# RG-LRU layer of a hybrid diffusion step on one core: unsplit float32 gates, the decay on ScalarE, a new pace table and x7 ahead of g6

## Chip, core and metric

The kernel runs on one core of a Trainium2 chip. The metric is the device time of one execution in microseconds, as the median of several runs. Engines are named as in the profile: PE (TensorE), PEld (its weight loads), DVE (VectorE), ACT (ScalarE), POOL (GpSimd), SP (SyncE, which issues most transfers).

## What is computed

One inference step of a two-layer backbone on 128 context and 512 latent tokens with 1024 channels. Layer 0 (SSD and differential attention) and both ConvFFNs are untouched. Layer 1 mixes with a bidirectional RG-LRU, all in float32:

```python
def rglru_direction(xr, wa, ba, wx, bx, lam, h0, reverse):
    xb = xr.reshape(b, n, RNN_BLOCKS, RNN_BLOCK_W)          # 16 blocks of 64 channels
    r = jax.nn.sigmoid(jnp.einsum('blnk,nkj->blnj', xb, wa).reshape(b, n, D_RNN) + ba)
    i = jax.nn.sigmoid(jnp.einsum('blnk,nkj->blnj', xb, wx).reshape(b, n, D_RNN) + bx)
    log_a = -RG_C * r * jax.nn.softplus(-lam)
    a = jnp.exp(log_a)
    u = jnp.sqrt(-jnp.expm1(2.0 * log_a)) * (i * xr)
    hseq, hlast = linear_scan(a, u, h0)                     # h[t] = a[t] h[t-1] + u[t]

def odd_mixer(h, w_in, conv_w, conv_b, wa, ba, wx, bx, lam, w_out, ctx):
    gate, xr = jnp.split(h @ w_in, 2, axis=-1)
    xr = dwconv_centred(xr, conv_w, conv_b)                 # width 4
    yf, hf = rglru_direction(xr, ..., h0f, False)
    yb, hb = rglru_direction(xr, ..., h0b, True)
    return ((yf + yb) * jax.nn.gelu(gate)) @ w_out, (hf, hb)
```

## The kernel before

Activations lie with channels on the 128 partitions and tokens on the free axis: 128 context tokens, a gap of 4 and 512 latent tokens make 644 columns (`NT`). The 1024 channels are 8 tiles. A float32 matrix product is done as three products of float32r parts (`mm3`): a weight and an operand are each split into a high part (a ScalarE cast) and a low part (a subtraction, for weights on GpSimd in pieces of 256 columns: the tiles `whi` and `wlo`, line 117), and high x high, high x low and low x high are added up in PSUM.

In the odd layer (`odd`) TensorE goes through 16 input projections, each of 8 x 2 x 3 = 48 products of 322 columns: for tile t the recurrent channels (called x0 to x7 here) and the gate channels (g0 to g7), in the order x0 g0 x1 g1 ... x7 g7 (`lru_order`). After an x block `recur` starts the tile's chain, after a g block `gelu`. Three weights are kept ready ahead of use.

The chain of a tile, for both directions d: the convolution `xr` (first tap on ScalarE, three on VectorE), its split into `xh` and `xl`, the split of the tile's gate weights `bd` into `bh` and `bl` (GpSimd), the gate products into the PSUM banks `mt` (two of them, 322 columns each), their Tanh on ScalarE into the tiles `t0` and `t1` (the profile calls both `t`), `decay` (Exp and Tanh on ScalarE, into `inv` and `t`), `forms` (five VectorE operations), `roots` (a square root on ScalarE, a product on GpSimd in three pieces), `scan` (one on VectorE for each direction), the addition of the two directions on GpSimd (three pieces, `pieces`, line 69), and `gated`, the product with the GELU. Most VectorE operations here go through one helper, line 317, so groups are told apart by tile names.

What runs when is set by ticks. `tick` is called as products are issued, once for each set of three in some loops and with 2 for each two sets in others, so a projection is 16 ticks; `after(n, f)` puts f into the program n ticks later. Every engine works off its instructions in the order in which the program issued them. The table `LRU` (and `LRU_LAST` for tile 7) holds the distances in ticks from the x block to the parts of its chain.

At the end of the layer `give_h` splits the gated tiles 0 to 6 into `H`, the operand of the output projection, as soon as the last gate block no longer needs H; the projection starts with the products that need H[0] to H[5], waits for H[6] and last for H[7].

Of the kernel before, what the change touches and what calls it, by code (L numbers as in the profile page):

```python
# [16 lines left out]
KD = D // 128  # L17
# [33 lines left out]
LRU_LAST = (9, 7, 14, 3, 7, 4, 4, 4)  # L51
LRU = (9, 9, 27, 3, 10, 7, 8, 6)
# [188 lines left out]
def tile_hybrid_step(ctx: ExitStack, tc: tile.TileContext, a, o):  # L241
# [184 lines left out]
    lru_order = [(what, t) for t in range(8) for what in "xg"]  # L426
# [1239 lines left out]
    def odd():  # L1666
        with ExitStack() as st:
# [35 lines left out]
            gys = {}  # L1703

            def recur(t, ps):

                xr = conv(pool, ps, "lru_cw", "lru_cb", 4, t, 8, "xr", 3)
                v = Core()

                def parts():  # L1710
                    v.xp = (pool.tile([128, NT], F32R, name="xh", tag="xh", bufs=2),
                            pool.tile([128, NT], F32R, name="xl", tag="xl", bufs=2))
                    split_into(v.xp, xr)

                def blocks():
                    b = bd[t % 2]
                    v.bh = pool.tile([128, 2, 2, 128], F32R, name="bh", tag="bh", bufs=2)
                    v.bl = pool.tile([128, 2, 2, 128], F32R, name="bl", tag="bl", bufs=2)
                    nc.scalar.copy(v.bh, b)
                    nc.gpsimd.tensor_sub(v.bl, b, v.bh.bitcast(F32))  # L1720
                    if t < 6:
                        gates_in(t + 2)

                hs = []

                def product(d, i):
                    if i == 0:
                        hs.append([])
                    w = tmp("t%d" % i, 4)
                    hs[d].append(w)  # L1730
                    for c0, c1 in HALVES:
                        ps = mtile()
                        mm3(ps, (v.bh[:, d, i], v.bl[:, d, i]), v.xp, c0, c1, 0, True, True)
                        nc.scalar.activation(w[:, c0:c1], ps[:, :c1 - c0], AF.Tanh, scale=0.5,
                                             bias=col(hba if i == 0 else hbx, d, t))

                def decay(d):
                    t1 = hs[d][0]
                    inv, e = tmp("inv", 2), tmp("e", 4)
# [21 lines left out]
                def scan(d):  # L1761
# [30 lines left out]
            def gelu(t, ps):  # L1792
                g = gys[t] = tmp("gy", 8)
# [167 lines left out]
```

## Time and profile before

| | |
|---|---|
| median of 3 runs | 2131.27 us (2123.99 to 2131.78) |
| profiled execution | 2128.0 us, span 2126.2 us |
| busy over the span | PE 1891.4 (89%), PEld 1735.7 (82%), DVE 1467.3 (69%), POOL 1208.1 (57%), ACT 964.2 (45%) |
| mean granted TensorE clock | 0.951 |
| HBM | 187.50 MB read, 6.92 MB written |

The shares are means over stages of different kinds. The odd layer lies between about 1322 and 1618 us of the span; times below are microseconds from the start of the span. A matmul's duration in the profile overlaps with the next one's, so the rate is read from the distance of two starts.

### The profile page before, as it was taken

What the parts mean: (1) busy time and instruction counts of PE and PEld (TensorE: products, weight loads), DVE (VectorE), ACT (ScalarE), POOL (GpSimd) and SP (SyncE); (2) the same over time, 40 slices, a digit from 0 to 9 for tenths busy, and PEclk for the clock granted to TensorE, in tenths of its full rate; (3) what the DMA queues carried; (4) which work ended last, traced back from release to release, by engine and by line L of the source; (5) the groups of instructions that cost most, each with busy time, mean ns of one, the idle gap of its engine ahead of it and who ended that gap; (6) DMA issues with size and microseconds to landing.
All of it is one profiled execution on the core that took longest, in us unless ns stands there. A gap on an engine that the chain in (4) does not pass through costs nothing.

```text
span 2126.2 us, 33767 instructions
## 1 busy us (share of the span) xinstructions
PE 1891.4 (89%) x12665; PEld 1735.7 (82%) x12665; DVE 1467.3 (69%) x2486; ACT 964.2 (45%) x1671; POOL 1208.1 (57%) x1542
## 2 busy tenths in 40 slices
PE   6878889999999988999999997977778799999997
PEld 4767768888888878799889997977678799999986
DVE  3477755656664357687777876788857778777874
ACT  3454444454553334343333444766724444343445
POOL 3335454333343535466666775688755577766772
PEclk9889999999999999999999998989789899999998
DMA  9545432121113431444542222111111122222221
GB/s 267 165 156 164 149 110 63 49 54 48 49 45 124 131 117 64 136 130 153 178 145 70 60 84 79 53 39 45 40 50 41 37 79 82 86 76 70 60 85 65
DMA packets 255578, 196.60 MB, mean 92 GB/s; under 512 B 13837, under 2 KB 233816, under 8 KB 255288
## 3 DMA queue, kind: packets, MB, share of 16 engines
q1 hardware_dynamic: 252664, 184.59, 28.9%
q0 software_dynamic: 2528, 7.13, 1.4%
q8 instruction: 100, 1.64, 0.3%
q10 hardware_dynamic: 224, 2.73, 0.3%
q14 instruction: 62, 0.51, 0.1%
HBM read 187.50 MB, written 6.92 MB: 91 GB/s over the span
## 4 chain that ended last, share of the span: by engine, by line
PE 36%; DVE 11%; POOL 9%; ACT 4%; issue 4%; DMA 4%; POOLq 0%; DVEq 0%; ACTq 0%; SPq 0%
PE wide L470 10%; PE wide L471 10%; PE wide L472 10%; POOL t L69 4%; POOL wlo L117 4%; DMA wraw<-in_ffn_w_up_dram 4%; DVE ft L317 2%; PE mt L332 1%; PE gh L470 1%; DVE X L317 1%; PE gh L471 1%; PE gh L472 1%; DVE wsum L141 1%; DVE wraw L140 1%; DVE wsum L139 1%
## 5 line engine op out<-in xcount | busy, mean ns | idle before, releaser
L117 POOL TENSOR_TENSOR wlo<-wraw,whi 128x256 fp32r<-128x256 f32 (+1 forms) x845 | 715.7, 875 | 544.7 <-ACT whi L112 476.8
L470 PE MATMUL wide<-hhi,whi 128*128 128x322 f32 (+4 forms) x1072 | 352.5, 329 | 49.5 <-DVE X L317 23.0
L471 PE MATMUL wide<-hlo,whi 128*128 128x322 f32 (+4 forms) x1072 | 345.8, 323 | 3.7 <-DVE hlo L511 3.4
L472 PE MATMUL wide<-hhi,wlo 128*128 128x322 f32 (+4 forms) x1072 | 343.1, 320 | 0.0
L112 ACT CAST whi<-wraw 128x1024 fp32r<-128x1024 f32 (+2 forms) x263 | 220.1, 839 | 150.4 <-PE wide L472 71.9
L470 PEld LDWEIGHTS wide<-hhi,whi 128*128 128x128 f32 x1072 | 213.2, 199 | 66.4 <-issue 21.6
L470 PE MATMUL gh<-hhi,whi 128*128 128x322 f32 (+3 forms) x704 | 236.7, 336 | 9.1 <-ACT zt L1160 8.6
L471 PE MATMUL gh<-hlo,whi 128*128 128x322 f32 (+3 forms) x704 | 221.2, 314 | 1.3 <-DVE hlo L511 1.0
L472 PE MATMUL gh<-hhi,wlo 128*128 128x322 f32 (+3 forms) x704 | 220.5, 313 | 0.0
L471 PEld LDWEIGHTS wide<-hlo,whi 128*128 128x128 f32 x1072 | 212.6, 198 | 6.1 <-DVE hlo L511 5.3
L472 PEld LDWEIGHTS wide<-hhi,wlo 128*128 128x128 f32 x1072 | 212.4, 198 | 0.0
L470 PE MATMUL wide<-hidh,whi 128*128 128x322 f32 (+4 forms) x624 | 199.7, 320 | 2.2 <-DVE ft L1584 2.2
L471 PE MATMUL wide<-hidl,whi 128*128 128x322 f32 (+4 forms) x624 | 195.5, 313 | 1.6 <-DVE hidl L511 1.6
L472 PE MATMUL wide<-hidh,wlo 128*128 128x322 f32 (+4 forms) x624 | 195.4, 313 | 0.0
L317 DVE SCALAR_TENSOR_TENSOR ft<-ft,PC 128x643 f32<-128x643 f32 x160 | 168.2, 1072 | 37.3 <-ACT ft L1526 35.3
L470 PEld LDWEIGHTS gh<-hhi,whi 128*128 128x128 f32 (+1 forms) x704 | 134.0, 190 | 34.7 <-issue 21.3
L1526 ACT ACTIVATE ft<-ft,PC 128x644 f32<-128x644 f32 x80 | 74.0, 927 | 144.4 <-DVE ft L1591 133.4
L317 DVE SCALAR_TENSOR_TENSOR X<-wide,modc,X 128x128 f32<-128x128 f32 (+3 forms) x264 | 123.5, 511 | 19.8 <-PE wide L472 19.8
L471 PEld LDWEIGHTS gh<-hlo,whi 128*128 128x128 f32 (+1 forms) x704 | 133.8, 190 | 2.4 <-DVE hlo L511 1.2
L472 PEld LDWEIGHTS gh<-hhi,wlo 128*128 128x128 f32 (+1 forms) x704 | 133.6, 190 | 0.6
L470 PEld LDWEIGHTS wide<-hidh,whi 128*128 128x128 f32 x624 | 118.7, 190 | 15.9 <-issue 7.0
L112 ACT CAST shi<-wsum 128x512 fp32r<-128x512 f32 x120 | 72.8, 617 | 124.3 <-DVE wsum L141 111.4
(386 smaller groups left out, 4676.4 us busy)
## 6 DMA issues: line engine op xcount, KB each, us to landing
wraw<-in_ffn_w_up_dram SPq DMA_DIRECT2D x88, 512.0 KB
mraw<-in_w_mod_dram SPq DMA_DIRECT2D x80, 512.0 KB
wraw<-in_ssd_attn_w_in_dram SPq DMA_DIRECT2D x42, 512.0 KB
wraw<-in_ffn_w_down_dram SPq DMA_DIRECT2D x96, 192.0 KB
E<-ad SPq DMA_DIRECT2D x16, 640.0 KB
mraw<-in_w_mod_dram SPq DMA_DIRECT2D x32, 256.0 KB
wraw<-in_ssd_attn_w_out_dram SPq DMA_DIRECT2D x16, 512.0 KB
wraw<-in_lru_w_in_dram SPq DMA_DIRECT2D x16, 512.0 KB
```

The source lines that it names most:

```text
L69: getattr(eng, op)(out[:, c], a[:, c], b[:, c])
L112: self.nc.scalar.copy(hi, src)
L117: low.tensor_sub(lo[:, q], src[:, q], hi[:, q].bitcast(F32))
L139: v.tensor_sub(s[:, 1], a[:, :4], b[:, :4])
L140: v.tensor_add(b[:, :4], b[:, :4], b[:, 4:])
L141: v.tensor_sub(s[:, 0], b[:, :4], a[:, :4])
L317: nc.vector.scalar_tensor_tensor(out, in0, scalar, in1, op0=op0, op1=op1, **kw)
L332: nc.tensor.matmul(m[32 * j:32 * j + 32, :256], scp[:, kt, :], raw[:, j * 256:(j + 1) * 256], start=half is None or kt == 0, stop=half is ...
L470: nc.tensor.matmul(ps[:whi.shape[-1], p0:p0 + c1 - c0], whi, xhi[:, c0:c1], start=start, stop=False)
L471: nc.tensor.matmul(ps[:whi.shape[-1], p0:p0 + c1 - c0], whi, xlo[:, c0:c1], start=False, stop=False)
L472: nc.tensor.matmul(ps[:whi.shape[-1], p0:p0 + c1 - c0], wlo, xhi[:, c0:c1], start=False, stop=stop)
L1526: after(at, lambda: nc.scalar.activation(out, u, AF.Identity, scale=par(cw, 2 * NF + t), bias=par(cb, t)))
```

## The change

The gate products are no longer split: one float32 product of `xr` with `bd` takes the place of three, and `xh`, `xl`, `bh`, `bl` with their casts and subtractions are gone. `bd` has three tiles in turn instead of two, and is refilled after the last product that reads it. The fifth operation of `forms` leaves VectorE: `e` becomes 2 `inv` - 1, an Identity with scale 2 and bias -1 on ScalarE, in a part of its own, `factors`, together with the GpSimd product. The inner part of the GELU is one VectorE operation where two were, with the constant moved into the scale of the Tanh; the GELU has a tile `gl` of its own, and the sum of the directions gets a tile `gy`. `t0`, `t1` and `e` have six buffers instead of four, `inv` three instead of two. The pace tables now count from the x block to each part, and spread the parts of one tile over the 32 ticks of an x and a g block. x7 comes ahead of g6. The last gate block is cut at the columns at which the output projection is cut.

```diff
-LRU_LAST = (9, 7, 14, 3, 7, 4, 4, 4)
-LRU = (9, 9, 27, 3, 10, 7, 8, 6)
+LRU_LAST = (10, 18, 4, 7, 12, 33, 41, 46)
+LRU = (14, 31, 4, 7, 14, 51, 59, 66)
...
-    lru_order = [(what, t) for t in range(8) for what in "xg"]
+    lru_order = [(what, t) for t in range(7) for what in "xg"]
+    lru_order[13:] = [("x", 7), ("g", 6), ("g", 7)]
...
-            k.n_sqt, k.sq_tag = 4, "t0"
+            k.n_sqt, k.sq_tag = 6, "t0"
...
-                def parts():
-                    v.xp = (pool.tile([128, NT], F32R, name="xh", tag="xh", bufs=2),
-                            pool.tile([128, NT], F32R, name="xl", tag="xl", bufs=2))
-                    split_into(v.xp, xr)
-
-                def blocks():
-                    b = bd[t % 2]
-                    v.bh = pool.tile([128, 2, 2, 128], F32R, name="bh", tag="bh", bufs=2)
-                    v.bl = pool.tile([128, 2, 2, 128], F32R, name="bl", tag="bl", bufs=2)
-                    nc.scalar.copy(v.bh, b)
-                    nc.gpsimd.tensor_sub(v.bl, b, v.bh.bitcast(F32))
-                    if t < 6:
-                        gates_in(t + 2)
...
-                    w = tmp("t%d" % i, 4)
+                    w = tmp("t%d" % i, 6)
                     hs[d].append(w)
                     for c0, c1 in HALVES:
                         ps = mtile()
-                        mm3(ps, (v.bh[:, d, i], v.bl[:, d, i]), v.xp, c0, c1, 0, True, True)
+                        nc.tensor.matmul(ps[:, :c1 - c0], bd[t % 3][:, d, i], xr[:, c0:c1], start=True, stop=True)
                         nc.scalar.activation(w[:, c0:c1], ps[:, :c1 - c0], AF.Tanh, scale=0.5,
                                              bias=col(hba if i == 0 else hbx, d, t))
+                    if d and i and t < 5:
+                        gates_in(t + 3)
...
                 def forms(d):
                     t1, t2, inv, e = hs[d]
-                    fma(t2, t2, 1.0, xr, op0=OP.add, op1=OP.mult)
                     nc.vector.tensor_scalar(inv, inv, 0.5, 0.5, op0=OP.mult, op1=OP.add)
                     fma(e, t1, 1.0, inv, op0=OP.subtract, op1=OP.mult)
                     fma(inv, e, 2.0, inv, op0=OP.add, op1=OP.mult)
+                    fma(t2, t2, 1.0, xr, op0=OP.add, op1=OP.mult)
+
+                def factors(d):
+                    t1, t2, inv, e = hs[d]
+                    nc.scalar.activation(e, inv, AF.Identity, scale=2.0, bias=minus)
                     pieces(nc.gpsimd, "tensor_mul", t2, t2, inv)
-                    fma(e, t1, 1.0, inv, op0=OP.add, op1=OP.mult)
...
-                    pieces(nc.gpsimd, "tensor_add", hs[0][0], hs[0][0], t1)
+                    y = gys[t] = tmp("gy", 8)
+                    pieces(nc.gpsimd, "tensor_add", y, hs[0][0], t1)
...
                 for d in range(2):
-                    at = pace[0] + pace[1 + d]
+                    at = pace[d]
                     after(at, lambda d=d: product(d, 0))
-                    after(at + 1, lambda d=d: product(d, 1))
-                    after(at + 2, lambda d=d: decay(d))
-                    at += 2 + pace[3 + d]
-                    after(at, lambda d=d: forms(d))
-                after(at + pace[5], roots)
-                after(at + pace[5] + pace[6], lambda: scan(0))
-                after(at + pace[5] + pace[6], lambda: scan(1))
-                after(at + pace[5] + pace[6] + pace[7], gated)
+                    after(at + 2, lambda d=d: product(d, 1))
+                    after(at + pace[2], lambda d=d: decay(d))
+                    after(at + pace[3], lambda d=d: forms(d))
+                    after(at + pace[4], lambda d=d: factors(d))
+                after(pace[5], roots)
+                after(pace[6], lambda: scan(0))
+                after(pace[6] + 1, lambda: scan(1))
+                after(pace[7], gated)
...
-                nc.vector.tensor_scalar(g, g, c * 0.044715, c, op0=OP.mult, op1=OP.add)
-                nc.vector.tensor_mul(g, g, ps)
-                after(5, lambda: nc.scalar.activation(g, g, AF.Tanh))
-                after(7, lambda: fma(g, g, 1.0, ps, op0=OP.add, op1=OP.mult))
+                fma(g, g, 1 / 0.044715, ps, op0=OP.add, op1=OP.mult)
+
+                def end():
+                    fma(g, g, 1.0, ps, op0=OP.add, op1=OP.mult)
+                    opened[t] = g
+                after(5, lambda: nc.scalar.activation(g, g, AF.Tanh, scale=c * 0.044715))
+                after(7, end)
...
-                for c0, c1 in HALVES:
+                k.cut = Cut(CUTS[2])
+                for c0, c1 in k.cut.parts:
...
-            until(lambda: k.n_given == 12)
+            until(lambda: k.n_given >= 7)
```

What this does to the order of the engines, at three places. On TensorE, one direction's first gate in the middle of the layer (`mt` is the gate's PSUM bank, `wide` the bank of a projection), before:

```order
L470 MATMUL mt<-xh,bh 128x322
L471 MATMUL mt<-xl,bh 128x322
L472 MATMUL mt<-xh,bl 128x322
L470 MATMUL mt<-xh,bh 128x322
L471 MATMUL mt<-xl,bh 128x322
L472 MATMUL mt<-xh,bl 128x322
L470 MATMUL wide<-hhi_76,whi 128x322
L471 MATMUL wide<-hlo_84,whi 128x322
L472 MATMUL wide<-hhi_76,wlo 128x322
```

and in the changed kernel:

```order
L473 MATMUL wide<-hhi_80,wlo 128x322
L1719 MATMUL mt<-xr,bd_13313 128x322 x2
L471 MATMUL wide<-hhi_81,whi 128x322
L472 MATMUL wide<-hlo_89,whi 128x322
L473 MATMUL wide<-hhi_81,wlo 128x322
L471 MATMUL wide<-hhi_81,whi 128x322
L472 MATMUL wide<-hlo_89,whi 128x322
L473 MATMUL wide<-hhi_81,wlo 128x322
L1719 MATMUL mt<-xr,bd_13313 128x322 x2
```

Six products of split parts have become two unsplit ones, and the same number of projection products stands between a gate and the next.

On GpSimd, from the second direction's product with the root to the addition of the directions (`t<-t,t` is the product with the root, `t<-t,inv` the multiplication of the next direction or tile, `wlo` a projection weight's low part), before:

```order
L69 TENSOR_TENSOR t_14131<-t_14131,t_14113 128x214
L69 TENSOR_TENSOR t_14131<-t_14131,t_14113 128x215 x2
L1758 MEMSET e 128x4
L1759 MEMSET t_14131 128x4
L69 TENSOR_TENSOR t_14225<-t_14225,inv 128x214
L69 TENSOR_TENSOR t_14225<-t_14225,inv 128x215 x2
L69 TENSOR_TENSOR t_13979<-t_13979,t_14113 128x214
L69 TENSOR_TENSOR t_13979<-t_13979,t_14113 128x215 x2
L117 TENSOR_TENSOR wlo<-wraw,whi 128x256 x4
L1720 TENSOR_TENSOR bl<-bd_13313,bh 128x512
```

and in the changed kernel:

```order
L69 TENSOR_TENSOR t_14249<-t_14249,t_14221 128x214
L69 TENSOR_TENSOR t_14249<-t_14249,t_14221 128x215 x2
L1749 MEMSET e 128x4
L1750 MEMSET t_14249 128x4
L69 TENSOR_TENSOR gy<-t_14105,t_14221 128x214
L69 TENSOR_TENSOR gy<-t_14105,t_14221 128x215 x2
L69 TENSOR_TENSOR t_14322<-t_14322,inv 128x214
L69 TENSOR_TENSOR t_14322<-t_14322,inv 128x215 x2
L117 TENSOR_TENSOR wlo<-wraw,whi 128x256 x4
```

The addition has moved ahead of the next multiplication, directly behind the products that the scan needs, and `bl` is gone.

On ScalarE, from the second direction's decay to the next tile's first gates (`inv` and the `t` with `lcols` are the decay, `t<-mt` the gates' Tanh, `whi` a weight cast, `gl` or `gy` from `wide` the GELU's Square), before:

```order
L1740 ACTIVATE inv<-t_14569,lcols 128x644
L1741 ACTIVATE t_14569<-t_14569,lcols 128x644
L507 CAST xh<-xr 128x644
L112 CAST whi<-wraw 128x1024
L1794 ACTIVATE gy<-wide 128x644
```

and in the changed kernel:

```order
L1728 ACTIVATE inv<-t_14221,lcols 128x644
L1729 ACTIVATE t_14221<-t_14221,lcols 128x644
L1741 ACTIVATE e<-inv,minus 128x644
L1720 ACTIVATE t_14309<-mt,lcols 128x322 x2
L1720 ACTIVATE t_14322<-mt,lcols 128x322 x2
L112 CAST whi<-wraw 128x1024
L1787 ACTIVATE gl<-wide 128x644
```

`xh` is gone, `e` has come, and the next tile's gates now stand between it and the weight cast.

## Rows read from the trace of the kernel before

**Rows 1.** Busy time in four stretches: length, each engine, granted clock, DMA share, GB/s.

```profile
1340.13:1371.57 31.44, 29.91 (x187) 28.85 (x186) 26.53 (x41) 22.37 (x33) 20.76 (x24) 1.00 0.28 76
1371.57:1479.53 107.96, 82.74 (x484) 79.17 (x483) 91.72 (x96) 69.00 (x97) 92.88 (x115) 0.89 0.16 44
1453.19:1479.53 26.34, 20.90 (x122) 19.91 (x121) 22.96 (x25) 16.63 (x25) 22.75 (x29) 0.87 0.21 60
1479.53:1561.67 82.14, 52.67 (x260) 48.04 (x258) 67.32 (x78) 45.92 (x71) 64.30 (x87) 0.77 0.09 27
```

**Rows 2.** Chain of waits, 1459 to 1480 us: start, length, engine, tile, line.

```profile
1466.84 1.48 POOL bl L1720
...
1473.06 0.53 ACT t L1734
...
1476.01 1.28 ACT L1755
1477.30 0.75 ACT t L1755
1478.19 2.25 POOL t L69 x3
```

**Rows 3.** Groups of TensorE, 1453.19 to 1479.53: busy, mean ns; idle before, releaser.

```profile
L472 PE MATMUL mt<-xh,bl 128*128 128x322 f32 x8 | 3.3, 410 | 2.9 <-POOL bl L1720 2.9
L470 PE MATMUL mt<-xh,bh 128*128 128x322 f32 x8 | 3.2, 398 | 1.0 <-ACT t L1734 0.9
L471 PE MATMUL mt<-xl,bh 128*128 128x322 f32 x8 | 3.1, 383 | 1.5 <-DVE xl L511 1.5
```

**Rows 4.** Groups of GpSimd in the same stretch.

```profile
L117 POOL TENSOR_TENSOR wlo<-wraw,whi 128x256 fp32r<-128x256 f32 x8 | 8.2, 1056 | 0.0
...
L69 POOL TENSOR_TENSOR t<-t,t 128x214 f32<-128x214 f32 x3 | 2.3, 773 | 1.9 <-ACT t L1755 1.9
L69 POOL TENSOR_TENSOR t<-t,inv 128x214 f32<-128x214 f32 x2 | 1.9, 934 | 1.7 <-DVE inv L317 1.7
```

**Rows 5.** Timeline of GpSimd and VectorE at quiet places: start, length, instruction.

```profile
1342.04 2.85 POOL L117 TENSOR_TENSOR wlo<-wraw,whi 128x256 fp32r<-128x256 f32 x4 [2.66 <-ACT whi L112]
...
1408.70 1.85 POOL L69 TENSOR_TENSOR t<-t,t 128x214 f32<-128x214 f32 x3
...
1365.89 0.50 DVE L1747 TENSOR_SCALAR inv<-inv 128x644 f32<-128x644 f32 x1 [0.78 <-ACT inv L1740]
...
1367.72 0.83 DVE L317 SCALAR_TENSOR_TENSOR inv<-e,inv 128x644 f32<-128x644 f32 x1
...
1386.09 1.56 DVE L1768 TENSOR_TENSOR_SCAN t<-e,PC,t 128x644 f32<-128x644 f32 x1 [0.95 <-POOL t L1759]
```

**Rows 6.** A group of VectorE, 1453.19 to 1479.53.

```profile
L511 DVE TENSOR_TENSOR xl<-xr,xh 128x644 fp32r<-128x644 f32 x1 | 1.3, 1347 | 0.0
```

**Rows 7.** Timeline of TensorE, split products, first and seventh start.

```profile
1348.36 0.31 PE L470 MATMUL wide<-hhi,whi 128*128 128x322 f32 x1
...
1349.25 0.31 PE L470 MATMUL mt<-xh,bh 128*128 128x322 f32 x1
```

**Rows 8.** Timeline of TensorE, float32 products of the attention and what follows.

```profile
619.21 1.06 PE L1307 MATMUL oo<-v,pt 128*128 128x128 f32 x8
620.10 0.61 PE L1307 MATMUL oo<-pv,pt 128*128 128x128 f32 x4
620.64 0.70 PE L1262 MATMUL wide<-fk,fq 64*128 64x512 f32 x2
```

**Rows 9.** Groups of ScalarE, 1453.19 to 1479.53.

```profile
L1734 ACT ACTIVATE t<-mt,lcols 128x322 f32<-128x322 f32 x8 | 4.0, 529 | 7.3 <-PE mt L472 7.3
...
L1740 ACT ACTIVATE inv<-t,lcols 128x644 f32<-128x644 f32 x2 | 1.8, 916 | 0.0
...
L1794 ACT ACTIVATE gy<-wide 128x644 f32<-128x644 f32 x1 | 0.7, 697 | 0.0
```

**Rows 10.** Timeline of GpSimd: an addition directly behind the products with the root.

```profile
1387.73 2.66 POOL L69 TENSOR_TENSOR t<-t,t 128x214 f32<-128x214 f32 x3 [1.68 <-DVE t L1768]
```

More of the change, by code (lines that the diff above doesn't have):

```diff
@@ L1671, in odd @@
             pool = k.tmp = lctx.enter_context(tc.tile_pool(name="lru", bufs=1))
-            k.n_sqt, k.sq_tag = 4, "t0"
+            k.n_sqt, k.sq_tag = 6, "t0"
             norm_part(1, 1, 0)
-            bd = [pool.tile([128, 2, 2, 128], F32, name=f"bd{i}") for i in range(2)]
+            bd = [pool.tile([128, 2, 2, 128], F32, name=f"bd{i}") for i in range(3)]
             for b in bd:
@@ L1677, in odd @@
             cols = pool.tile([128, 6, 2, 8], F32, name="lcols")
+            minus = pool.tile([128, 1], F32, name="minus")
             cb = [cols[:, i].rearrange("p d t -> p (d t)") for i in range(6)]
@@ L1693, in gates_in @@
             def gates_in(t):
-                b = bd[t % 2]
+                b = bd[t % 3]
                 for i, nm in enumerate(("lru_wa", "lru_wx")):
@@ L1770, in scan @@
                     nc.vector.tensor_copy(last[:, 1, t:t + 1], t1[:, 0:1])
-                    pieces(nc.gpsimd, "tensor_add", hs[0][0], hs[0][0], t1)
+                    y = gys[t] = tmp("gy", 8)
+                    pieces(nc.gpsimd, "tensor_add", y, hs[0][0], t1)
                 def gated():
-                    fma(gys[t], hs[0][0], 0.5, gys[t], op0=OP.mult, op1=OP.mult)
-                    k.scanned = t + 1
+                    if t not in opened:
+                        after(1, gated)
+                        return
@@ L1777, in recur @@
+                    fma(gys[t], gys[t], 0.5, opened.pop(t), op0=OP.mult, op1=OP.mult)
+                    k.scanned.add(t)
                 pace = LRU_LAST if t == 7 else LRU
-                after(1, blocks)
-                after(pace[0], parts)
                 for d in range(2):
-                    at = pace[0] + pace[1 + d]
+                    at = pace[d]
                     after(at, lambda d=d: product(d, 0))
-                    after(at + 1, lambda d=d: product(d, 1))
-                    after(at + 2, lambda d=d: decay(d))
-                    at += 2 + pace[3 + d]
-                    after(at, lambda d=d: forms(d))
@@ L1799, in gelu @@
-                after(7, lambda: fma(g, g, 1.0, ps, op0=OP.add, op1=OP.mult))
-            gates_in(0)
-            gates_in(1)
+                fma(g, g, 1 / 0.044715, ps, op0=OP.add, op1=OP.mult)
[4 more added lines that the diff above has]
+                after(7, end)
+            for t in range(3):
+                gates_in(t)
@@ L1803, in sink @@
+            nc.gpsimd.memset(minus, -1.0)
             def sink(what, t):
@@ L1810, in give_h @@
             def give_h(t, c0, c1):
-                if k.scanned <= t:
+                if t not in k.scanned:
                     after(1, lambda: give_h(t, c0, c1))
@@ L1826, in last_gate @@
                         W.ahead()
-                        gelu(7, p[:, OFF:OFF + NT])
+                        gelu(7, p[:, k.cut.off:k.cut.off + NT])
                     for t in range(7):
@@ L1831, in odd @@
             last_gate()
-            until(lambda: k.n_given == 12)
+            until(lambda: k.n_given >= 7)
             hctx = ExitStack()
-            k.cut = Cut(CUTS[2])
             def ready():
@@ L1851, in then @@
                     until(lambda: k.fresh[0])
-            out_parts(H, evac, then, wide_banks, [[0, 1], [2]], [lambda: until(lambda: k.scanned > 6 and k.n_given == 14), ready], 3)
+            out_parts(H, evac, then, wide_banks, [[0, 1], [2]], [lambda: until(lambda: len(k.scanned) == 8 and k.n_given == 14), ready], 3)
             W.over = None
```

10 lines of the change are left out of this document (4 added, 6 removed).

## Prediction

> **What bounds the kernel now.** The change touches the odd layer alone, so I first cut the trace into stretches. Where one tile's recurrent channels leave TensorE is marked by the ScalarE instruction that starts their convolution, and those marks are the ends of the stretches in [rows 1]. From tile 2 to tile 6 the kernel takes 107.96 us for four tiles, 27.0 each; one of them, 26.34 us, stands there alone. The reader should see that no engine is full in it: TensorE 20.90, VectorE 22.96, GpSimd 22.75, ScalarE 16.63. So it is either a ring of waits or something shared.
>
> Both are there. The chain of waits [rows 2] goes round once a tile: GpSimd works without a break up to the end of `bl`, 1468.32; TensorE's gate products follow until ScalarE takes over at 1473.06; ScalarE runs to the square root, and GpSimd starts again at 1478.19. The gate products stand in TensorE's order in front of the projections, so each of their waits stops the whole engine: 2.9 us for `bl`, 1.5 for `xl`, 0.9 for ScalarE to empty the bank [rows 3], and the engine is at the lower of its two levels, 1.2 instead of 2.4 GHz, for part of the time (granted clock 0.87 in that stretch [rows 1]).
>
> The shared thing shows in durations. With VectorE quiet or on PSUM, GpSimd does four weight pieces in 2.85 us (0.71 each) and three chain pieces in 1.85 (0.62); VectorE alone takes 0.83 for an operation on two SBUF tensors, 0.50 for one with a constant, 1.56 for a scan [rows 5]. In the stretch the weight piece takes 1.06 on average [rows 4], and `xl`, of the 0.83 kind, 1.35 [rows 6]. They hold each other up, so an operation removed on one engine also shortens the other.
>
> **The change, part by part, per tile.** *TensorE.* 24 split products go, 8 unsplit float32 ones come. Split ones start 0.148 apart: six starts from 1348.36 to 1349.25 [rows 7]; 24 are 3.6 us. No float32 product of 322 columns is in the trace. As the lower bound I take the three split ones that it stands for, 0.44; the nearest rows are the attention's float32 products, 12 records for six products of 128 columns in 1.43 us, 0.119 a record, two records each [rows 8]: by columns 0.60 for 322 at full clock, twice that at the lower one. I take 0.60, since the engine idles less: 8 x 0.60 = 4.8, 1.2 more a tile. It has cover: projections 96 x 0.148 = 14.2, with the gates 19.0 of a 26.3 us interval. The waits for `xl` and `bl` (4.4) cannot recur, the operands are gone.
>
> *VectorE.* Of the kind that collides there are now ten operations of 0.83 (`xl`, two `t`, six on `e` and `inv`, the gating), three constant ones and two scans: 8.3 + 1.5 + 3.1 = 12.9 us. `xl`, the two closing `e` and one constant operation of the GELU go: 9.9. The new GELU operation reads PSUM like the multiplication it replaces.
>
> *ScalarE.* Two casts of 644 and 512 columns go, nearest to the Square's 0.70 and by columns 0.56; two Identity operations come, nearest to the 0.92 of the Exp of the same shape [rows 9]: +0.6, hidden in an engine that waits 7.3 us a tile for gate products [rows 9]. But `e` now stands in its queue ahead of the next Tanh pair, and waits for VectorE: see the slower rival.
>
> *GpSimd.* `bl` goes. Undisturbed, its list was 8 x 0.71 + 15 x 0.62 + memsets 0.4 + `bl` 1.4 (two pieces) = 16.8 us and took 22.75 [rows 1]: 6.0 lost to VectorE's 12.9, 0.465 a microsecond. Now: 15.4 + 0.465 x 9.9 = 20.0. Its order gives a wait: the addition stands directly behind the products that feed the second scan, where the old order had the next tile's multiplication between. Where that happened before, the wait was 1.68 [rows 10]; I add 1.7. Of its old waits, 1.7 for `inv` and 1.9 for the square root [rows 4], the first has seven ticks more and goes; half of the second I keep, 0.9, as the root still follows Exp, Tanh and a table load. Sum 22.6 an interval, against bounds of 19.0 (TensorE full) and 26.3 (all given back). Four: 90.4, **17.6 us less**.
>
> The Trainium skill's page "SBUF — State Buffer", section "SBUF: two separate sides", says that a VectorE operation with two SBUF inputs and a GpSimd operation that reads SBUF hold a port pair exclusively, whole instructions at a time. The rows bear out the collision but not the full lock: by it the old interval would need 12.9 + 16.8 = 29.7, and 26.3 was measured. By it the new interval is 9.9 + 15.4 = 25.3, a rival below.
>
> *Head, tiles 0 to 2.* TensorE is busy 29.91 of 31.44 us [rows 1]; 12 unsplit products replace 36: 7.2 - 5.3 = +1.9, and the 1.5 us not busy go: **+0.4**. Three bd tiles instead of two mean one more memset and four more small loads ahead of time, on GpSimd and on SyncE's queue while both wait for the norm: nothing. A later refill of bd waits in SyncE's queue for the last product that reads it; the weight loads behind it are three blocks early, so that too is hidden. The larger count of gate buffers takes away a wait that hardly exists: nothing either way.
>
> *Tail, from tile 6 to the first product that needs H[7].* 82.14 us now [rows 1], TensorE busy 52.67 of it. x7 ahead of g6 gives the last chain two projections as cover instead of one, and the gate of tile 7 is cut at the output projection's own cut, so that six H tiles are split while TensorE still works. I count GpSimd's new list from the mark of x6: 16 weight pieces and 42 chain pieces, 11.4 + 26.0 + 0.8 = 38.2. VectorE's colliding work beside it: five sets of forms at 2.99, six scans, three gatings, six H splits (0.83 each in two parts) = 31.9, x 0.465 = 14.8. Waits: 1.7 before tile 5's addition and 1.7 before tile 7's; the roots of tile 7 stand behind g7's Square and a table load, 0.70 + 1.28 + 0.75 = 2.7 [rows 2, 9]; the end, two gatings, cast and split, 0.83 + 0.83 + 0.7 + 0.83 = 3.2. Three weights are kept ahead, so up to two splits, 5.7, may still queue at the mark. Sum 68.0: **14.1 us less**. Bounds: 50 if TensorE decides (21.3 of projections, 20 gate products 12.0, then roots 2.7, twelve pieces 7.4, scan 1.6, addition 1.9, end 3.2), 82 if nothing is won.
>
> Sum: -17.6 - 14.1 + 0.4 = -31.3. The profiled execution was 2128.0 us (span 2126.2 and 1.8 around it): 2096.7. It lies 3.3 below the median of the runs, 2131.27; placing the new median half that above, I get **2098**.
>
> **The rivals.** (a) *Another ring closes.* From one tile to the next follow each other: the six product pieces 3.7, scan 1.6, convolution (three operations like the 0.83 ones) 2.5, gating 0.8, three forms 2.2, `e` 0.9, three gate Tanh at 0.53, Square 0.7, and ScalarE's stretch up to the next root, 5.1 [rows 2]: 19.1. Stretched as `xl` is (1.35 for 0.83), VectorE's 7.1 become 11.5; with hand-overs of some 0.1 to 0.2 that is 25. For it: VectorE works in order and is nearly full. Against: only if every part waits for the one before it. Then 4 x 25 is -8 in the intervals, and about -8 in the tail: **2114**.
> (b) *Full lock between VectorE and GpSimd*: four intervals of 25.3 are 101.2, -6.8; tail 38.2 + 31.9 + 3.2 = 73.3, -8.8; +0.4: **2114**. Against: the old interval would not fit, 29.7 in 26.3. It is the rule of the page of the Trainium skill named above.
> (c) *TensorE becomes the bound*: intervals of 20, tail near 60: -28 - 22: **2080**. For it: its own list is 19.0; against: GpSimd's 20.0 without any wait.
> (d) *Slower: ScalarE's order.* `e` waits twice a tile for three VectorE operations, 3.2 us each when disturbed, and the Tanh that empties the gate bank stands behind it; TensorE stops there. ScalarE's 16.6 + 0.6 with these 6.4 on top of its present 7.3 is 30.9 an interval: +16, tail unchanged, **2145**. It decides once ScalarE's waits pass 9.8 us a tile (27.0 - 17.2). Against: `e` is due seven ticks after its inputs.
> (e) *Nothing won*: the order of the tail eats what the intervals give, 2121 to 2142.
>
> **How the numbers follow.** A measurement of this kernel can tell about 0.5% from no change: 2120.6 and 2141.9 are the limits. Forecast 0.54 (its own range 2083 to 2108), (a) 0.20, (b) 0.07, (c) 0.06, (e) 0.08, (d) 0.05. Faster: the forecast, (c) and most of (a) and (b), 0.83; same 0.12; slower 0.05. The range 2080 to 2120 leaves out (d), (e), half of (c) and a little of (a): 0.18.
>
> **What would show it.** Right: between the marks of tiles 2 to 6 about 22.6 us; no wait of TensorE above 1 us at a gate product; granted clock near 1.0; weight pieces below 1.0 us; a wait of 1.7 before each `gy` addition; 68 us from the mark of x6 to H[7]. Wrong: float32 products above 0.7 us; long waits of ScalarE for `inv` in front of `e`; intervals above 25, or below 20 with TensorE full.

## The result: 0.9918 of the time before, and the profile after

The changed kernel takes 2111.94 us (median of 4 runs, 2106.64 to 2115.64) against 2130.98 for the kernel before (4 runs on the same chip). The ratio is 0.9918, with a 95% interval of 0.9899 to 0.9938: 17 to 19 us faster, where 31.3 were forecast. The profiled span is 2109.2 us, 17.0 less than the 2126.2 of before. I give the parts of that difference in the prediction's own stretches.

Windows of the changed kernel, cut at the same marks as [rows 1] (length, busy time of TensorE, its weight loads, VectorE, ScalarE, GpSimd, granted clock, DMA share, GB/s): head, four tiles, one of them, tail.

```profile
1338.83:1373.14 34.31, 32.86 (x183) 29.29 (x181) 22.78 (x36) 23.07 (x34) 17.81 (x25) 1.00 0.24 66
1373.14:1471.90 98.76, 83.34 (x450) 74.86 (x449) 68.80 (x78) 70.72 (x97) 80.60 (x115) 0.91 0.18 49
1424.37:1448.97 24.60, 21.25 (x112) 19.37 (x111) 17.78 (x21) 16.78 (x24) 19.70 (x28) 0.86 0.17 48
1471.90:1541.87 69.97, 43.49 (x225) 37.96 (x223) 57.30 (x67) 42.27 (x68) 60.38 (x79) 0.87 0.10 31
```

Head +2.9 us (forecast +0.4), four tiles -9.2 (forecast -17.6), tail -12.2 (forecast -14.1). The first mark comes 1.3 earlier, and from H[7] to the end of the span it is 567.3 us instead of 564.5, 2.8 longer. Together: -17.0. No run here isolates the last two; among all runs below the stretch behind H[7] lies between 563.7 and 567.7. Each stretch is read from one profiled execution. Run 9 below, which differs from the changed kernel in the order of the last projections alone, takes 100.08 us for the four tiles instead of 98.76, so 1 to 2 us between two stretches tell nothing.

GpSimd does what was forecast (80.60 / 4 = 20.1 us a tile, forecast 20.0). What went otherwise is waiting. Groups of the 24.60 us tile, to be held against [rows 3, 9]: TensorE, then ScalarE (busy us, mean ns | idle just before, releaser).

```profile
L1719 PE MATMUL mt<-xr,bd 128*128 128x322 f32 x16 | 6.4, 521 | 3.3 <-ACT t L1720 3.3
L1741 ACT ACTIVATE e<-inv,minus 128x644 f32<-128x644 f32 x2 | 1.6, 824 | 6.0 <-DVE inv L317 6.0
L1720 ACT ACTIVATE t<-mt,lcols 128x322 f32<-128x322 f32 x8 | 4.0, 527 | 1.7 <-PE mt L1719 1.7
```

GpSimd's three groups that wait, over the four tiles, to be held against [rows 4]:

```profile
L117 POOL TENSOR_TENSOR wlo<-wraw,whi 128x256 fp32r<-128x256 f32 x32 | 32.6, 1052 | 4.2 <-ACT whi L112 4.2
L69 POOL TENSOR_TENSOR t<-t,t 128x214 f32<-128x214 f32 x10 | 7.5, 753 | 3.4 <-ACT t L1746 3.4
L69 POOL TENSOR_TENSOR gy<-t,t 128x214 f32<-128x214 f32 x4 | 2.6, 648 | 10.6 <-DVE t L1759 10.6
```

An engine's busy time and waits always fill its stretch; here they show the size of each term. By tile it is 20.15 of work, 1.05 for `whi`, 0.85 for the root and 2.65 before the addition, 24.7 in all. The forecast's 22.6 had 20.0, nothing, 0.9 and 1.7. The addition waited 1.68 us in three of the tiles, as forecast, and 5.54 in the first. What these waits hang on shows in the timeline of the 24.60 us tile (start, length, instruction, idle before it):

```profile
1421.86 3.05 POOL L69 TENSOR_TENSOR t<-t,t 128x214 f32<-128x214 f32 x3
1425.02 1.56 DVE L1759 TENSOR_TENSOR_SCAN t<-e,PC,t 128x644 f32<-128x644 f32 x1 [0.37 <-POOL t L1750]
1426.70 2.73 DVE L317 SCALAR_TENSOR_TENSOR xr<-wide,PC,xr 128x642 f32<-128x642 f32 x3
1429.35 1.07 DVE L317 SCALAR_TENSOR_TENSOR gy<-gy,gl 128x644 f32<-128x644 f32 x1
1432.59 1.24 DVE L317 SCALAR_TENSOR_TENSOR inv<-e,inv 128x644 f32<-128x644 f32 x1
1433.86 0.83 ACT L1741 ACTIVATE e<-inv,minus 128x644 f32<-128x644 f32 x1 [5.99 <-DVE inv L317]
1434.60 0.93 ACT L1720 ACTIVATE t<-mt,lcols 128x322 f32<-128x322 f32 x2
1435.16 2.52 PE L1719 MATMUL mt<-xr,bd 128*128 128x322 f32 x4 [3.35 <-ACT t L1720]
1438.14 1.03 ACT L112 CAST whi<-wraw 128x1024 fp32r<-128x1024 f32 x1
1439.26 1.43 POOL L117 TENSOR_TENSOR wlo<-wraw,whi 128x256 fp32r<-128x256 f32 x2 [1.78 <-ACT whi L112]
```

GpSimd's products with the root release VectorE's scan; the next convolution, the gating and the forms stand behind that scan; `e` on ScalarE waits 5.99 us for `inv`; the Tanh that empties a gate bank stands behind `e`; TensorE waits 3.35 for that Tanh; the weight cast stands behind the Tanh, and GpSimd waits for the cast. After its stop TensorE runs at the lower of its two levels for a while (granted clock 0.50 from 1435.16 to 1440.00): four records of gate products take 2.52 us there and 1.25 elsewhere.

This goes round. The part of the turn that comes before the timeline above begins at TensorE's previous wait for the same Tanh:

```profile
1410.84 2.51 PE L1719 MATMUL mt<-xr,bd 128*128 128x322 f32 x4 [3.36 <-ACT t L1720]
1418.55 1.37 ACT L1746 ACTIVATE t<-t 128x644 f32<-128x644 f32 x2
1419.44 2.39 POOL L69 TENSOR_TENSOR t<-t,t 128x214 f32<-128x214 f32 x3 [0.74 <-ACT t L1746]
```

The last of these gate products lets its Tanh start at 1413.39. From there ScalarE works without a pause through the weight cast, the GELU's Square, the decay and a table load to the two roots at 1418.55. The first root releases GpSimd's six product pieces, and these release the scan at the top of the timeline above. From 1410.84 to 1435.16 one turn takes 24.32 us: about 2.6 on TensorE, 5.9 and 1.3 on ScalarE, 5.5 on GpSimd, 8.8 on VectorE, and hand-overs.

### The profile page after: what moved, and what is told of

It is laid out like the page before. It is cut to its first block, busy times and chain, and to the rows that moved or that the text cites. A ratio compares the mean times of both kernels' runs of the same rounds, so it can differ in the third digit from the quotient of the medians.

```text
span 2109.2 us, 33582 instructions
## 1 busy us (share of the span) xinstructions
PE 1890.8 (90%) x12601; PEld 1728.1 (82%) x12601; DVE 1431.1 (68%) x2454; ACT 963.7 (46%) x1670; POOL 1188.8 (56%) x1536
## 5 line engine op out<-in xcount | busy, mean ns | idle before, releaser
L471 PE MATMUL wide<-hhi,whi 128*128 128x322 f32 (+4 forms) x1072 | 360.2, 336 | 49.9 <-DVE X L317 22.9
```

Source lines behind the costliest of these rows:

```text
L471: nc.tensor.matmul(ps[:whi.shape[-1], p0:p0 + c1 - c0], whi, xhi[:, c0:c1], start=start, stop=False)
```

## Experiments

**Theory 1** on seeing this: `e`, put into ScalarE's queue ahead of the next Tanh, closes a ring, and TensorE pays with a stop a tile. **Rival 2:** GpSimd's list decides, and the waits are slack. All ratios below are to the kernel before, 5 or 6 timed runs for each (4 for the last). The diffs show the main lines of each edit.

**1. `e` later.**

```diff
-nc.scalar.activation(e, inv, AF.Identity, scale=2.0, bias=minus)
+after(0 if t == 7 else 4, lambda: nc.scalar.activation(e, inv, AF.Identity, scale=2.0, bias=minus))
```

> The changed kernel with `e` on ScalarE four ticks later, behind the next direction's two gate Tanh instead of ahead of them. Theory 1 (ScalarE's order closes the ring: `e` waits 6.0 us for `inv`, the gate Tanh stands behind it, TensorE stops 3.3 us at a gate product and then runs at the low clock): TensorE's wait at gate products falls below 1 us a tile, granted clock 1.00, the four intervals x2 to x6 go from 98.8 to 90 to 94 us, the total 5 to 9 us below the changed kernel, ratio to the kernel before 0.987 to 0.990. Rival 2 (GpSimd's own list decides, 19.7 to 20 us and its waits of 1.7 and 1.4, the wait of ScalarE is only slack): the waits move elsewhere, intervals within 1 us in all of 98.8, ratio 0.991 to 0.993. Rival 3 (the later `e` delays the square root that follows it): intervals over 100, ratio over 0.994.

Measured 0.9891 (0.9876 to 0.9907), 2104.9 us; four tiles 93.15, tail 69.74. As Theory 1 had it in sum, but not in the waits, which it wanted below 1 us a tile. TensorE's group over the four tiles, the changed kernel first, then this one:

```profile
L1719 PE MATMUL mt<-xr,bd 128*128 128x322 f32 x65 | 24.6, 504 | 15.4 <-ACT t L1720 13.8 <-issue 1.6
```

```profile
L1719 PE MATMUL mt<-xr,bd 128*128 128x322 f32 x64 | 22.7, 481 | 13.7 <-issue 9.2 <-ACT t L1720 4.5
```

The wait for ScalarE fell from 13.8 to 4.5, and 9.2 put down to "issue" have come. The timeline at the longest of these shows for what:

```profile
1397.41 0.15 DVE L1755 COPY t<-PC 128x1 f32<-128x1 f32 x1 [2.50 <-POOL t L1750]
1400.48 1.56 DVE L1759 TENSOR_TENSOR_SCAN t<-e,PC,t 128x644 f32<-128x644 f32 x1 [0.95 <-POOL t L1750]
1402.17 2.73 DVE L317 SCALAR_TENSOR_TENSOR xr<-wide,PC,xr 128x642 f32<-128x642 f32 x3
1405.00 1.41 PE L1719 MATMUL mt<-xr,bd 128*128 128x322 f32 x2 [6.62 <-issue]
```

The product starts 0.1 us after the convolution that makes its `xr`, and the convolution stood behind the scan. So VectorE is late, and two things on TensorE's path wait for it. It is late here because it stood still itself, 2.50 and 0.95 us ahead of the two scans, for GpSimd's products with the root; GpSimd had come to these without a pause, behind four weight pieces that took 4.58. Where neither wait is long, as in the third of these tiles, an interval is 19.83 us with TensorE busy 19.08 and its clock at 1.00. That isn't a rate that lasts: GpSimd has 39 instructions in the long tile before it and 23 in this one, and the two take 47.96 together:

```profile
1394.61:1422.74 28.13, 20.80 (x107) 18.17 (x106) 18.97 (x22) 16.66 (x25) 24.11 (x39) 0.82 0.22 61
1422.74:1442.57 19.83, 19.08 (x114) 17.27 (x113) 16.31 (x20) 16.68 (x25) 17.90 (x23) 1.00 0.16 44
```

**2. The addition later**, behind the next multiplication on GpSimd, and **3. both moves**.

```diff
-pieces(nc.gpsimd, "tensor_add", y, hs[0][0], t1)
+after(0 if t == 7 else 1, lambda: pieces(nc.gpsimd, "tensor_add", y, hs[0][0], t1))
```

> The changed kernel with GpSimd's addition of the two directions one tick later, behind the next multiplication, so that its wait of 1.7 us for the second scan is covered. Theory 1: the 1.7 us come back as a longer wait for the weight cast `whi` (1.8 us now), which hangs on TensorE; four intervals 98 to 99 us, ratio as the changed kernel, 0.991 to 0.993. Rival 2 (GpSimd decides): 1.7 us less a tile, four intervals 92 us, ratio 0.988 to 0.989.

> Both moves together. Theory 1: with ScalarE's order mended GpSimd is next, 20.0 us and little waiting, so that the addition's 1.7 us now count: four intervals 86 to 90 us, ratio 0.984 to 0.988, about the 2098 us that were forecast. Rival 2: no more than the addition alone gives, 92 us.

Alone 0.9929 (0.9915 to 0.9942), four tiles 101.17, where Theory 1 had 98 to 99. As it said, the 1.7 us were not what decides: the wait before the addition is gone, and GpSimd waits 7.7 us for `whi` instead of 4.2, and 7.0 ahead of the multiplications. Both 0.9887 (0.9868 to 0.9906), four tiles 93.98, the same as the later `e` alone; the tail is 66.52, 3.2 shorter, but the ratios can't be told apart. So the forecast for both, 86 to 90, fell: with `e` mended GpSimd's wait still counts for nothing in the four tiles.

**4. `e` on VectorE.**

```diff
-nc.scalar.activation(e, inv, AF.Identity, scale=2.0, bias=minus)
+fma(e, t1, 1.0, inv, op0=OP.add, op1=OP.mult)
```

> The changed kernel with `e` back on VectorE as (t+1)*inv, at the same place in the program; nothing of the recurrence is left on ScalarE between the decay and the next Tanh pair. Theory 1: TensorE's wait of 3.3 us at a gate product goes, but VectorE has two operations of 0.83 more that collide with GpSimd (0.465 x 1.66 = 0.8 us a tile): four intervals 92 to 96 us, tail 2 us longer, ratio 0.989 to 0.991. Rival 2: intervals 0.8 longer each, 102 us, tail 2 us longer, ratio 0.994 to 0.995.

Measured 0.9900 (0.9883 to 0.9917), tail 72.81 as expected, but four tiles 97.83, more than the 92 to 96. The group of waits says why:

```profile
L1719 PE MATMUL mt<-xr,bd 128*128 128x322 f32 x67 | 24.8, 498 | 15.9 <-issue 14.6 <-ACT t L1720 1.2
```

ScalarE's 13.8 are gone, and the wait for the convolution has taken their whole place. In all three of these waits on "issue" (9.01, 2.63 and 2.92) the product starts 0.1 us after the convolution. ScalarE's order was one of two doors, and VectorE stands behind both. In the longest wait VectorE had again stood still for GpSimd's products, 2.49 and 0.95 us.

**5. Scans later**, and **6. with the later `e`**.

```diff
-after(pace[6], lambda: scan(0))
-after(pace[6] + 1, lambda: scan(1))
-after(pace[7], gated)
+late = 12 if t < 6 else 0
+after(pace[6] + late, lambda: scan(0))
+after(pace[6] + late + 1, lambda: scan(1))
+after(pace[7] + late, gated)
```

> The changed kernel with both scans and the gating of tiles 0 to 5 twelve ticks later, so that in VectorE's order they stand behind the next tile's convolution and the forms of the running tile instead of ahead of them; `e` stays where it was. Theory 1, as the run with the later `e` left it (what comes late is VectorE, which stands still at the scan until GpSimd has done the products with the root, and the convolution, the forms, `e` and the gate products are all queued behind that scan): TensorE's waits at gate products for ScalarE (3.3 us a tile) and for the convolution (the 6.6 us put down to issue in the run with the later `e`) both fall below 1 us, four intervals 82 to 89 us, ratio 0.982 to 0.987. Rival 2 (ScalarE's order of `e` and Tanh is a ring of its own): four intervals 95 to 99 us, ratio 0.990 to 0.993. Rival 3 (the later scan delays the gating and so the tail, or holds buffers longer): tail over 73 us, ratio over 0.993.

> Both the later scans and the later `e`. Theory 1: with VectorE on time `e` no longer waits, so that its place is worth little: within 3 us of the run with the later scans alone, four intervals 82 to 88 us, TensorE or GpSimd full. Rival 2: the two gains add, 5 us or more below the later scans alone.

Measured 0.9912 (0.9897 to 0.9928) and 0.9903 (0.9888 to 0.9918): no gain on the changed kernel that these intervals can tell. The windows (four tiles and tail of 5, then of 6):

```profile
1372.13:1464.34 92.21, 79.23 (x450) 71.53 (x448) 67.63 (x76) 70.62 (x97) 80.34 (x109) 0.96 0.17 46
1464.34:1539.70 75.36, 46.37 (x225) 40.95 (x223) 56.98 (x68) 42.92 (x68) 61.26 (x85) 0.79 0.13 36
```

```profile
1374.81:1465.01 90.20, 81.03 (x454) 72.89 (x454) 70.08 (x78) 71.35 (x98) 79.33 (x108) 0.94 0.18 48
1465.01:1542.76 77.75, 43.39 (x218) 37.88 (x218) 57.00 (x69) 42.58 (x68) 60.83 (x87) 0.83 0.12 34
```

TensorE's waits at the gate products of the four tiles, 5 and then 6, and what VectorE waits for in 5:

```profile
L1719 PE MATMUL mt<-xr,bd 128*128 128x322 f32 x65 | 22.5, 467 | 13.0 <-ACT t L1720 10.8 <-issue 2.1
L1719 PE MATMUL mt<-xr,bd 128*128 128x322 f32 x64 | 23.4, 494 | 9.2 <-ACT t L1720 5.6 <-issue 3.4
L317 DVE SCALAR_TENSOR_TENSOR gy<-gy,gl 128x644 f32<-128x644 f32 x4 | 5.0, 1260 | 9.6 <-POOL gy L69 9.6
```

Theory 1 for 5 wanted both waits nearly gone and four tiles of 82 to 89. With the scans out of the way 10.8 of the changed kernel's 13.8 us for the Tanh are still there, and VectorE stands still at another place, the gating, for GpSimd's addition.

The second reaches the forecast 90.4 for the four tiles, and the tail is 7.8 us longer than in the changed kernel. That is the tail that Rival 3 had, though not its ratio. I read it so, without a run that isolates it: what the scans leave undone in the tiles has to be done behind the mark of x6, where TensorE has too little work to cover it. From x2 to H[7] the sums are 168.7 (changed), 162.9 (later `e`), 167.6 and 168.0. The intervals alone are no measure of this kernel.

**7. Split gates in the changed kernel**, with `parts` and `blocks` back, and four gate buffers. **8. Four buffers** with the unsplit gates. The first two lines are of 7 alone, the others of both.

```diff
-nc.tensor.matmul(ps[:, :c1 - c0], bd[t % 3][:, d, i], xr[:, c0:c1], start=True, stop=True)
+mm3(ps, (v.bh[:, d, i], v.bl[:, d, i]), v.xp, c0, c1, 0, True, True)
-w = tmp("t%d" % i, 6)
+w = tmp("t%d" % i, 4)
-inv, e = tmp("inv", 3), tmp("e", 6)
+inv, e = tmp("inv", 2), tmp("e", 4)
```

> The changed kernel with the gates split in three float32r products again (xh, xl, bh, bl made as before), and four gate buffers and two `inv` instead of six and three, since six don't fit beside the split ones; all else as changed. Theory 1 (the unsplit gates bring the interval's gain by GpSimd's `bl`, 1.4 us and its share of collisions, and VectorE's `xl`, 0.83 to 1.35): four intervals 103 to 108 us, nearly the 107.96 of before, tail 3 to 5 us longer, ratio 0.995 to 1.000. Rival 2 (the spread over 32 ticks brings it): four intervals within 2 us of 98.8, ratio 0.992 to 0.994.

> The changed kernel with four buffers for the gates and `e` and two for `inv`, as before, instead of six and three. It is also what the run with split gates is to be held against. Theory 1 (no instruction waits for these buffers): within 2 us of the changed kernel in the four intervals and in the tail, ratio 0.991 to 0.993. Rival 2 (the buffers are what let the gates spread, and the loss of the split version came from them): four intervals over 105 us, ratio over 0.996.

Split gates: 1.0057 (1.0042 to 1.0073), slower than before, four tiles 116.64, which neither theory had. Four buffers: 0.9939 (0.9926 to 0.9952), four tiles 102.97, of which the first is 29.48 instead of 24.64. In that tile of the kernel with four buffers:

```profile
L1720 ACT ACTIVATE t<-mt,lcols 128x322 f32<-128x322 f32 x8 | 3.9, 527 | 6.7 <-POOL gy L69 5.1 <-PE mt L1719 1.7
```

A gate Tanh waits 5.1 us for the buffer that the addition reads. It happens once, and by the ratios the two extra buffers are worth 4.5 us (0.0021), though the intervals overlap. Neither theory had that size right. Between 8 and 7 only the gates differ: 0.0118, 25 us for unsplit gates in the spread order. In 7 the split of `xr` comes five ticks ahead of the first gate, though, where the kernel before has nine. In the split version TensorE's waits over the four tiles are:

```profile
L472 PE MATMUL mt<-xl,bh 128*128 128x322 f32 x32 | 12.6, 392 | 20.1 <-DVE xl L512 17.3 <-DVE t L1769 2.9
L471 PE MATMUL mt<-xh,bh 128*128 128x322 f32 x32 | 12.2, 380 | 10.1 <-ACT xh L508 5.7 <-ACT t L1734 4.4
```

The longest wait is for VectorE again, now at `xl`; how much of it the five ticks make, no run shows.

**9. Old order of the last projections** (g6 ahead of x7).

```diff
-lru_order = [(what, t) for t in range(7) for what in "xg"]
-lru_order[13:] = [("x", 7), ("g", 6), ("g", 7)]
+lru_order = [(what, t) for t in range(8) for what in "xg"]
```

> The changed kernel with the old order of the last projections (g6 before x7), all else as changed. Theory 1 (x7 ahead of g6 gives the last chain a second projection as cover): from the mark of x6 to H[7] 74 to 80 us instead of 70.0, ratio 0.994 to 0.997. Rival 2 (the cut of the gate of tile 7 and the shorter lists alone shortened the tail): within 2 us, ratio 0.991 to 0.993.

Measured 0.9916 (0.9899 to 0.9932), tail 71.34: Rival 2. x7 ahead of g6 is worth nothing that can be told here.

**10. Unsplit gates alone, in the kernel before**, with three bd tiles.

```diff
-mm3(ps, (v.bh[:, d, i], v.bl[:, d, i]), v.xp, c0, c1, 0, True, True)
+nc.tensor.matmul(ps[:, :c1 - c0], bd[t % 3][:, d, i], xr[:, c0:c1], start=True, stop=True)
```

> The kernel before with one part of the change alone: unsplit float32 gates (xh, xl, bh and bl go, three bd tiles instead of two); its old order, its old pace and all else stay. Theory 1 (the part brings the whole gain by what leaves GpSimd and VectorE, as the changed kernel with split gates was 29 us slower): four intervals 92 to 100 us instead of 107.96, tail 76 to 80 instead of 82.1, ratio 0.990 to 0.994. Rival 2 (the part pays only with gates spread over 32 ticks): within 6 us of the kernel before, ratio 0.997 to 1.000.

Measured 0.9938 (0.9922 to 0.9954). Four tiles and tail, to be held against [rows 1]:

```profile
1371.94:1470.07 98.13, 84.27 (x465) 75.62 (x463) 83.70 (x90) 65.06 (x88) 86.46 (x108) 0.93 0.16 44
1470.07:1550.18 80.11, 50.20 (x225) 42.48 (x226) 66.19 (x79) 43.64 (x67) 64.16 (x87) 0.78 0.11 33
```

Theory 1 holds in the ratio and the four tiles. This one part gives the four tiles 9.8 us, as much as the whole change (9.2). All that the change does besides (two VectorE operations to ScalarE, the GELU, the spread, the buffers) added nothing there in sum, though VectorE is busy 68.80 instead of 83.70; its gain is in the tail, 80.11 to 69.97. The sum hides a gain and a loss. The first of the four tiles in run 10 and in the changed kernel:

```profile
1371.94:1400.10 28.16, 21.02 (x114) 18.98 (x113) 21.56 (x25) 18.22 (x26) 21.58 (x28) 0.88 0.09 24
1373.14:1397.78 24.64, 21.30 (x112) 19.41 (x111) 16.54 (x20) 20.84 (x29) 18.60 (x32) 0.86 0.12 33
```

The rest of the change gives 3.5 us in this tile and loses 4.2 in the other three (69.97 to 74.12); with the later `e` they take 70.30, so the loss goes with where `e` stood. Yet TensorE waits for ScalarE's Tanh in run 10 too, where no `e` is on ScalarE:

```profile
L1717 PE MATMUL mt<-xr,bd 128*128 128x322 f32 x68 | 24.5, 487 | 13.6 <-ACT t L1718 13.2 <-ACT whi L112 0.4
```

Of the 13.2 us 7.14 come at once, in the first tile, where the Tanh waits for a gate buffer. The other two waits are 3.0 each.

**11. The addition on VectorE**, with the later `e`, and **12. the last tile's second product with the root there too**.

```diff
-pieces(nc.gpsimd, "tensor_add", y, hs[0][0], t1)
+nc.vector.tensor_add(y, hs[0][0], t1)
```

and in 12, in `roots`:

```diff
-pieces(nc.gpsimd, "tensor_mul", t2, t2, t1)
+if t == 7 and t1 is hs[1][0]:
+    nc.vector.tensor_mul(t2, t2, t1)
+else:
+    pieces(nc.gpsimd, "tensor_mul", t2, t2, t1)
```

> The later `e`, and the addition of the two directions on VectorE, directly behind the second scan, instead of in three pieces on GpSimd. Theory 1, as it stands after the runs with later scans (GpSimd's list and its waits set the pace; VectorE, in order, stands behind it and TensorE behind VectorE): GpSimd loses 1.9 us of work and a wait of 1.7 a tile, VectorE gains 0.83 to 1.25; four intervals 82 to 88 us instead of 93.2, tail 65 to 68 instead of 69.7, ratio 0.981 to 0.985. Rival 2 (VectorE's own order is the limit): four intervals 92 to 96 us, ratio 0.988 to 0.991.

> As the run with the addition on VectorE, and for the last tile the second direction's product with the root on VectorE too, since GpSimd works through twelve pieces at the end of the tail while VectorE waits. Theory 1: another 2 to 3 us from the tail, ratio 0.980 to 0.984. Rival 2: the product queues behind the H splits on VectorE and the last scan comes no earlier, no difference to the run without it.

Measured 0.9848 (0.9830 to 0.9866), 2096.99 us, and 0.9853 (0.9838 to 0.9868): both beat the kernel before and the changed one, and can't be told from each other: the tail of 12 is 64.42, not 2 to 3 us shorter. How much of it is the addition's is less sure: by the ratios 9 us (0.9891 to 0.9848, from two sets of runs), by the profiled spans 2.2 (2101.5 to 2099.3). Windows of 11:

```profile
1373.40:1467.96 94.56, 81.18 (x452) 72.56 (x452) 72.01 (x84) 71.33 (x98) 76.15 (x107) 0.95 0.18 51
1467.96:1532.70 64.74, 43.26 (x221) 38.39 (x220) 56.57 (x71) 42.57 (x68) 49.36 (x64) 0.86 0.11 33
```

Tail 64.74 (5.0 less than with the later `e` alone), about as expected, and the ratio is Theory 1's. The four tiles stayed at 94.56 instead of 82 to 88, though GpSimd lost 4 us of work and its wait for the scan: here Rival 2 holds. GpSimd now waits for VectorE's forms:

```profile
L69 POOL TENSOR_TENSOR t<-t,inv 128x214 f32<-128x214 f32 x9 | 8.1, 896 | 13.6 <-DVE t L317 12.2 <-DVE t L1755 1.4
```

## Why the prediction was right in sign and too large in size

- **What was right.** Sign and range (2112 in 2080 to 2120), the range because it took in rivals (a) and (b): the forecast's own, 2083 to 2108, was missed. GpSimd's list, 20.0 forecast, 20.1 measured; the 1.7 wait before the addition, in three of the four tiles; the waits for `xl` and `bl`, which are gone; the tail, 70.0 against 68. Of its signs for being right, a clock near 1.0 (0.91 in the four tiles) and weight pieces below 1.0 us (1.05) did not come, and long waits of ScalarE for `inv`, a sign for being wrong, did.
- **The step that failed** is "Sum 22.6 an interval". It summed GpSimd's list and its own waits, as if GpSimd closed the interval, with nothing for `whi` (1.05 a tile) and too little before the addition (2.65 a tile). The timelines show why: a ring over all four engines closes, 24.32 us a turn, and GpSimd's six product pieces are 5.5 of it. TensorE's groups at gate products, over the four tiles of the kernel before, of which [rows 3] is one:

```profile
L470 PE MATMUL mt<-xh,bh 128*128 128x322 f32 x32 | 12.4, 387 | 11.3 <-ACT t L1734 9.3 <-ACT xh L507 1.9
L472 PE MATMUL mt<-xh,bl 128*128 128x322 f32 x32 | 12.3, 386 | 8.7 <-POOL bl L1720 8.7
L471 PE MATMUL mt<-xl,bh 128*128 128x322 f32 x32 | 11.8, 369 | 5.2 <-DVE xl L511 5.2
```

  They waited 25.2 us. In the changed kernel it is 15.4, and the 9.8 between these is about the gain (9.2), as TensorE's busy time hardly changed (82.74, 83.34). The forecast let the waits for `xl` and `bl` go, which they did (13.9), and took less in their place than came: the wait for ScalarE's Tanh grew from 9.3 to 13.8. Take that away, and the convolution takes its place (14.6 with `e` on VectorE).
- **Whose lateness.** No single engine's is shown. That it isn't ScalarE's order alone is shown by runs 1 and 4, where the convolution took over the wait (9.2 and 14.6), and by run 10, with 13.2 and no `e` on ScalarE. That it isn't VectorE's order alone is shown by run 5, with 10.8 left for the Tanh; and in the longest waits of 1 and 4 VectorE itself stood still for GpSimd. That mending the order is not enough is shown by 6: the forecast interval was reached and the tail took it back. What stays open is what would break the ring for good: no run here moved VectorE's scans without a longer tail, and none gave the gates more than their two PSUM banks.
- **Rival (d)**, ScalarE's order, named the place rightly: `e` waits 21.9 us over the four tiles. Its price was wrong by what it added up: the old waits of 7.3 a tile for gate products [rows 9] fell to 1.7, so ScalarE waits 7.7 in the tile shown, below the 9.8 from which (d) would decide.
- **Rival (a)**, the ring through VectorE and ScalarE with 25 us a tile and 2114 in all, named what happened: 24.7 and 2112. Its argument against, that it holds "only if every part waits for the one before it", was met: each does in the timelines above. That its 25 came so near is partly luck. It had 11.5 for VectorE's part (8.8 in the turn above), 3.7 for GpSimd's pieces (5.5), and no gate products (2.6).
- **Rival (b)**, the full lock, has the same 2114 in all, and needs 25.3 a tile (9.9 of VectorE's and 15.4 of GpSimd's). Run 6 went at 90.20 / 4 = 22.6, so the lock is not what decides. Collisions there are: operations of 0.83 when undisturbed [rows 5] took 1.07 and 1.24 in the timeline above. The Trainium skill's page "SBUF — State Buffer", section "SBUF: two separate sides", has a VectorE operation with two SBUF inputs and a GpSimd operation that reads SBUF shut each other out for whole instructions; by that rule run 6 could not have been below 25.3 a tile, and the measurement decides.
- **The head**, +2.9 instead of +0.4: I counted 12 unsplit products between x0 and x2. There are 16 (32 records, two a product), since the order brings gates of tile 1 forward, and TensorE is busy 32.86 us instead of 31.8. Their price was nearly right, and high rather than low. The other part is idle time: the 1.5 us that were to go are there again (34.31 less 32.86), 1.2 of them for ScalarE's Tanh.
- **The tail** came out near its forecast partly for a wrong reason. x7 ahead of g6 (run 9) gives nothing, and unsplit gates alone 2.0 of the 12.2. The other 10 belong to the lighter VectorE lists, the cut and the spread together. With `e` back on VectorE (run 4) the tail is 2.8 longer; no run divides the rest.
- **"Nothing either way"** for the gate buffers was wrong: one wait of 5.1 us (run 8). The trace of the kernel before had it, in the first of the four tiles:

```profile
1387.94 1.28 ACT L1734 ACT_TABLE_LOAD   x1 [5.60 <-DVE last L1770]
1390.43 0.95 ACT L1734 ACTIVATE t<-mt,lcols 128x322 f32<-128x322 f32 x2 [1.21 <-POOL t L69]
1391.01 0.63 PE L470 MATMUL mt<-xh,bh 128*128 128x322 f32 x1 [7.24 <-ACT t L1734]
```

  By these releasers ScalarE waits there until VectorE and GpSimd have read the `t` that the Tanh writes anew, and TensorE waits 7.24 us for the Tanh, most of the 9.3 above. The forecast read the last of the four tiles, where that wait is 0.9 [rows 3].

## What to carry to other kernels

When operands vanish, a wait at their place need not: ask which engine was late, and what else on the same path waits for that engine. A sum over one engine's list gives the interval only if none of its own inputs come round from its outputs. Where they do, add up the ring as well, engine by engine, before you put it aside. An instruction moved to a less busy engine can stand ahead of others that are urgent there: `e` four ticks later gave the four tiles 5.6 us. Read more than one turn of a loop, since the longest wait can be in another. Measure from the start of the loop to the end of its tail, since work pushed out of the loop comes back where nothing covers it.

## What the hardware showed unexpectedly

A float32 product of 322 columns costs 0.54 us at full clock, where 0.60 was scaled from narrower ones. Timeline of the changed kernel, two such products (four records) between split ones that start 0.175 apart:

```profile
1346.02 1.25 PE L1719 MATMUL mt<-xr,bd 128*128 128x322 f32 x4
1346.86 0.58 PE L471 MATMUL wide<-hhi,whi 128*128 128x384 f32 x1
1347.28 0.34 PE L472 MATMUL wide<-hlo,whi 128*128 128x384 f32 x1
```

From the start of the first to the start of the second split product behind them it is 1.26 us, less 0.175: 1.09 for two. Part of the price falls behind them: the split product that follows takes 0.58 instead of 0.34.
